# Attention values in portions of two query tiles, narrower first scores, and a last norm that goes tile by tile

## The chip, the cores and the metric

The kernel runs on one core of a Trainium2 chip. Such a core has five engines with instruction streams of their own: TensorE (PE) multiplies matrices into PSUM, VectorE (DVE) and ScalarE (ACT) do elementwise work, GpSimd (POOL) does small elementwise work and issues transfers, and SyncE (SP) issues transfers. They wait for one another by semaphores. The metric is the device time of one execution in microseconds (us). The program runs on one core, so the slowest core is the only one.

## The reference

One step of a decoder with one layer computes 512 prompt tokens and 8 x 8 sample tokens, 576 columns in all, at a width of 1024:

```python
h = _rmsnorm(x, norm1_g) * (1.0 + sc1) + sh1
proj = h @ w_in                       # b_gate, c_gate, xa, q, k, v, ga, gb
u = c_gate * xa
uc, new_conv = _causal_conv(u, conv_buf, conv_w)
ya = (b_gate * uc) @ w_conv_out
o, k_state, v_state = attend(q, k, v, attn_sinks)
yb = o @ w_attn_out
mixed = jax.nn.sigmoid(ga) * ya + jax.nn.sigmoid(gb) * yb
x = x + g1 * (mixed @ w_mix_out)
h2 = _rmsnorm(x, norm2_g) * (1.0 + sc2) + sh2
a, val = jnp.split(h2 @ w_up, 2, axis=-1)
ac, new_ffn = _causal_conv(a, ffn_buf, ffn_conv_w)
x = x + g2 * ((jax.nn.gelu(ac, approximate=False) * val) @ w_down)
...
y_prompt = _rmsnorm(xp, final_g)
y_sample = _rmsnorm(xs, final_g)
```

The attention of the prompt works in blocks of 128 queries. A block sees its own 128 keys and the 128 before them, with a distance penalty, a mask and a sink in the softmax; the first block has no keys before it:

```python
s = jnp.einsum('...qhgd,...khd->...hgqk', q, k) * (HEAD_DIM ** -0.5)
s = s - _alibi_slopes()[:, :, None, None] * dist[..., None, None, :, :]
s = jnp.where(valid[..., None, None, :, :], s, NEG_INF)
m = jnp.maximum(jnp.max(s, axis=-1, keepdims=True), sink)
p = jnp.exp(s - m)
p = p / (jnp.sum(p, axis=-1, keepdims=True) + jnp.exp(sink - m))
return jnp.einsum('...hgqk,...khd->...qhgd', p.astype(v.dtype), v)
```

There are 16 query heads of width 64 in 4 groups, each group with one key and value head.

## The kernel before

Activations lie transposed: 128 channels on the partitions, the 576 tokens along the free dimension, one tile for each of the eight channel blocks. Weights come from DRAM in blocks of eight 128 x 128 pieces (`load_w`, line 148). So that the products are as exact as float32, each operand is split into a high and a low part of the type fp32r (`split`, line 138: ScalarE copies the high part, VectorE subtracts), and each product is made in three passes, high x high, high x low and low x high (`kstep`, line 206). A plain `product` (line 218) does so for eight pieces and two column groups of 256 and 320 tokens (`GRP`). A `pair_product` (line 449) makes two output blocks of 128 channels at once by a scheme with seven parts in place of eight, on sums of weights and of activations; its columns are halves of 288 tokens. The weights of such a pair (a `Job`, line 1288) are made by `prepare` (line 1298) in steps named A, B, C and D, each with a high and a low part. For a letter in `moved` the low part is not a subtraction on VectorE: ScalarE writes the negated high part, and a transfer that GpSimd issues adds the raw weights to it (`low`, line 409).

The kernel goes through these stages: the first norm; the keys and values; six `PLAIN` blocks of the inner convolution (line 1429), made by plain products; 18 jobs of pair products; the attention's output products; the mixing; the second norm; the up-projections with their convolution; the down-projections; the final norm and the stores.

Beside the plain products runs a filler (`fill`, `tick`, lines 186 to 199): a generator that advances by a step for each so many pieces of a product. It holds the attention first (line 1149). `attention()` has 16 units, four key heads by four query blocks. At step n it makes the scores of unit n (`prompt_scores`, line 1095), advances by one yield, makes the values of unit n - 3 (`prompt_values`, line 1131) and turns the softmaxed scores of unit n - 2 (`prompt_turn`, line 1116). For the first unit of a head it waits until the head's queries are there and 8 ticks old.

- `prompt_scores` makes eight matmuls for a unit: four query heads, each with the high and with the low part of the keys. High and low parts of a query lie in the two halves of the partitions, which a transfer on GpSimd's queue puts there (`queries`, line 903). Each is 256 keys wide, for the first query block too, which has only 128 keys.
- `prompt_turn` transposes the scores, 128 x 128 at a time, into one or two tiles of 512 columns that ScalarE copies out of PSUM.
- `prompt_values` multiplies with the values. A weight piece is only 64 columns wide, so that two matmuls go to the two halves of the PSUM partitions. Float32 matmuls that are not fp32r are issued as two instructions each. A unit has two or four matmuls, 4 or 8 instructions; ScalarE then copies 256 columns into the attention's output tile `ot`.

PSUM is given out as two pairs of banks (`mmps`) and four single banks (`aux`). What sets the order: a planner orders the instructions of each engine by a simulated timeline. Instructions of engines in the list `pinned` are tied behind the one issued before on their engine; PE is in it from line 968, ScalarE and VectorE too from line 1465. The first matmul of `prompt_values` is not tied, so that the planner may place it, with everything tied behind it, ahead of scores that are not ready.

In the last plain step (line 1461) the weights of job 0 are prepared between the product's pieces. Each convolution of an inner block (`branch_conv`, line 1377) is one GpSimd copy, one ScalarE multiplication and two VectorE operations over 592 columns; that of block 6 is done in job 0, at step 3. Job 2 is its first reader.

At the end, the last two down-projection blocks are made in column groups of their own. `summed` (line 2071) squares an output block on ScalarE, adds the square to `acc3` on VectorE and scales the block by the norm's weight on ScalarE. `final_rows` (line 2083) sums `acc3` over the partitions by matmuls with a tile of ones, one for each token tile, and raises the sums to the power of -1/2 (`rows_rsqrt`, line 577: one VectorE and one GpSimd instruction). A `TokenTile` (line 1749) transposes a tile of 128 tokens back, `finish` scales it by that factor, 512 channels on ScalarE and 512 on VectorE, and stores both halves. Token tiles 2 and 3 are finished while the last product runs (`others`, line 2186). Token tile 4 holds the 64 sample tokens.

Of the kernel before, what the change touches and what calls it, by code (L numbers as in the profile page):

```python
# [16 lines left out]
P = 128  # L17
# [55 lines left out]
def step_kernel(ctx: ExitStack, tc: tile.TileContext, ins: dict, outs: list):  # L73
# [766 lines left out]
    def vt(i):  # L840
        return V[i // 2][:, i % 2, :]
# [253 lines left out]
    def prompt_scores(hd, i):  # L1095
        w = 256 if i else P
        k0 = (i - 1) * P if i else 0
        ss = [slot("s", shape=[P, 2, 256]) for _ in range(2)]
        kh, kl = (x[:, k0 : k0 + 256] for x in KS[hd])
        for x in range(2):  # L1100
            S = aux()
            for e in range(2):
                q = QS[4 * hd + 2 * x + e][:, i * P : i * P + P]
                dst = S[:, e * 256 : e * 256 + 256]
                matmul(dst, q, kh, start=True, stop=False)
                matmul(dst, q, kl, start=False, stop=True)
# [21 lines left out]
            pts.append(t)  # L1128
        return pts

    def prompt_values(hd, i, pts):
        nkt = len(pts)
        O = aux()
        for n in range(2 * nkt):
            kt, par = n // 2, n % 2
            done = nc.tensor.matmul(  # L1136
                O[HALF[par], :256],
                vt(i - nkt + 1 + kt)[:, hd * 64 : hd * 64 + 64],
                pts[kt][:, par * 256 : par * 256 + 256],
                start=(kt == 0), stop=(kt == nkt - 1),  # L1140
            )
            if n:
                tc.keep_in_program_order(done)
        nc.scalar.copy(
            ot[hd // 2][:, 2 * (hd % 2) : 2 * (hd % 2) + 2, i * P : i * P + P],
            O[:, :256].rearrange("p (g c) -> p g c", g=2),
        )

    def attention():
        units = [(hd, i) for hd in range(4) for i in range(4)]  # L1150
        s, pts = {}, {}
        for n in range(len(units) + 3):
            if n in CACHE_AT:
                cache_load(CACHE_AT.index(n))
            if n < len(units):
                hd, i = units[n]
                while 4 * hd + 3 not in QS or ticks[0] < ready[hd]:
                    yield False
                s[n] = prompt_scores(hd, i)
            yield False  # L1160
            if n >= 3:
                prompt_values(*units[n - 3], pts.pop(n - 3))
            if 2 <= n <= len(units) + 1:
                pts[n - 2] = prompt_turn(units[n - 2][1], s.pop(n - 2))
            yield False
        filler[1] = .35
        before = None
        for n in range(3):
            s, more = [], []
            if n < 2:  # L1170
                yield from decode_scores(n, s, more)
            if before is not None:
                yield from before
            before = decode_values(n, s, more)
# [254 lines left out]
    for at, m in enumerate(PLAIN):  # L1429
        if at in (4, 5):  # L1430
            src, dst = ((ins["cache_k_win"], nks), (ins["cache_v_win"], nvs))[at - 4]
            tc.keep_in_program_order(
                nc.gpsimd.dma_start(
                    dst[:, 0:120, :].rearrange("b (x w) c -> b x (w c)", x=2),
                    src[0].rearrange("b w h d -> b w (h d)")[:, 8:128, :].rearrange(
                        "b (x w) c -> b x (w c)", x=2
                    ),
                )
            )
        if 1 <= at <= 3:  # L1440
            key_parts(at)
            for t in (2 * at, 2 * at + 1):
                queries(t)
        w = weights(kpm(w_in, 1024 + m * P), NK)
        if at in (4, 5):
            operands(2 * at - 8)
        if at == 5 and filler:
            filler[1] = .4
        ps = product(w, h)
        if at == 0:  # L1450
            stT = state_in(st_conv, "stT", NK)
        if at == 1:
            a = aux()
            transpose(a[:, :74], par2, ident[:74, :74])
            nc.scalar.copy(par2T, a[:, :74])
        c_sb = slot("c")
        nc.scalar.copy(c_sb, ps)
        w = weights(kpm(w_in, 2048 + m * P), NK)
        if at in (4, 5):
            operands(2 * at - 7)  # L1460
        steps = {}
        if at == len(PLAIN) - 1:
            jobs[0].load()
        if at == len(PLAIN) - 1:
            pinned += [pe, act, dve]
            fs = [f for x in jobs[0].prepare("BD").values() for f in x]
            for k, n in [(0, 2), (1, 1), (2, 1), (3, 1), (4, 2), (5, 1), (6, 1), (7, 1)]:
                steps[k], fs = fs[:n], fs[n:]
            jobs[1].load()
        ps = product(w, h, steps)  # L1470
        u = padded()
        dve.tensor_tensor(out=u[:, 2:514], in0=pv(ps), in1=pv(c_sb), op=ALU.mult)
        dve.tensor_tensor(
            out=b10(u)[:, :, 2:10], in0=b8(sv(ps)), in1=b8(sv(c_sb)), op=ALU.mult
        )
        keep_state(u, m, NK)
        inner[m] = lambda u=u, m=m: branch_conv(u, m)
        if at < len(PLAIN) - 1:
            inner[m]()
# [9 lines left out]
    def g_list(names):  # L1489
        return [g_at(int(n[0]), n[1:]) for n in names.split()]  # L1490

    jobs[0].before = {2: [op.n3 for op in hp], 3: [lambda: inner[6]()]}
    jobs[7].before = {2: [lambda: inner[3]()]}
    jobs[8].before = {2: [lambda: inner[7]()]}
    jobs[9].before = {2: [lambda: state_out(NK, ncv_p[:], ncv_s[:])]}
# [253 lines left out]
    class TokenTile:  # L1749
# [14 lines left out]
        def finish(self, queues):  # L1764
            r, i = self.rows, self.i
            out = [slot("yo", shape=[P, 512]) for _ in range(2)]
            fr = r3[r, i : i + 1]
            act.activation(out[0][r], self.ps[0][r], AF.Copy, scale=fr)
            if i == 4:
                act.activation(out[1][r], self.ps[1][r], AF.Copy, scale=fr)  # L1770
            else:
                dve.tensor_scalar(
                    out=out[1][r], in0=self.ps[1][r], scalar1=fr, scalar2=None, op0=ALU.mult
                )
            for hh, queue in enumerate(queues):
                cs = slice(hh * 512, hh * 512 + 512)
                dst = y_p[0, i * P : i * P + P, cs] if i < 4 else y_s.flatten_outer_dims()[:, cs]
                queue.dma_start(dst, out[hh][r])
# [289 lines left out]
    acc3 = slot("acc")  # L2068
    r3 = cp.tile([P, 8], F32, tag="r3", name="r3")

    def summed(m, c0=0, c1=NT, last=False):

        sq = acc3 if m == 0 else slot("sq")
        act.activation(sq[:, c0:c1], x1[m][:, c0:c1], AF.Square)
        if m and not last:
# [5 lines left out]
        return sq  # L2081

    def final_rows(g, sq=None):

        a = mmps()
        i0, i1, step = (0, 2, 512) if g == 0 else (2, 5, 2)
        parts = [acc3] if sq is None else [acc3, sq]
        for n, x in enumerate(parts):
            for i in range(i0, i1):
                dst = a[:, (i - i0) * step : (i - i0) * step + 2]  # L2090
                matmul(dst, tok_cols(x, i), ones[:, 0:2], start=n == 0, stop=n == len(parts) - 1)
        src = a[:, : (i1 - i0) * step].rearrange("p (i e) -> p i e", e=step)[:, :, 0]
        rows_rsqrt(r3[:, i0:i1], src)
# [80 lines left out]
    def down_late(m, g, between=None):  # L2174
        ps = product_g(late[m - NK + LATE], fa, g, mmps(), between)
        residual(ps, x1[m], 40 + m, *GRP[g])
        return summed(m, *GRP[g], last=(m, g) == (NK - 1, 0))

    for m in range(NK - LATE, NK):
        down_late(m, 1)  # L2180
# [3 lines left out]
    pinned.extend([pe, act, dve])  # L2184

    def others():
        final_rows(1)
        for i in (2, 3):
            tt = TokenTile(i)
            tt.turn(range(NK))  # L2190
            tt.finish((nc.sync, nc.sync))

    sq = down_late(NK - 1, 0, (3, others))
    tt = TokenTile(4)
    tt.turn(range(NK))
    tt.finish((nc.sync, nc.sync))
    final_rows(0, sq)
    for i, last in ((0, nc.sync), (1, nc.scalar)):
        tt = TokenTile(i)
        tt.turn(range(NK))  # L2200
# [35 lines left out]
```

## Time and profile before

| what | value |
|---|---|
| median of three runs | 966.99 us (966.77 to 967.02) |
| the profiled execution | 968.06 us |
| its span | 966.2 us |
| mean granted TensorE clock | 0.996 of full speed |
| TensorE busy | 950.6 us, 98% |
| VectorE busy | 710.5 us, 74% |
| ScalarE busy | 540.9 us, 56% |
| GpSimd busy | 131.8 us, 14% |
| moved by transfers | 144.61 MB, mean 150 GB/s |

All times of the profile count from the start of the span. Engines: PE is TensorE's matmul stream and PEld its weight loads, which overlap the matmuls. A row of the timeline gives the start, the length, the engine, the line, the operation, output <- input, the shape and a count of merged instructions. In brackets, where there is one, stands how long the engine was idle before and what released it. Most operations are recorded by one helper and so have line 112; they are told apart by their tiles. Matmuls overlap, so that the time one of them takes from the others is read from start to start, not from its length. In the page, a line of 40 digits gives the busy share of an engine in 40 slices of the span, in tenths.

### The profile page before, as it was taken

How to read it: one execution, taken by the hardware profiler on the slowest of the kernel's cores; microseconds unless marked ns; L12 is line 12 of the kernel's file. 1: busy time of each engine (PE TensorE's matmuls, PEld its weight loads, DVE VectorE, ACT ScalarE, POOL GpSimd, SP SyncE). 2: the span in 40 equal slices, each digit the busy share in tenths (PEclk: the TensorE clock that was granted, in tenths of full speed). 3: DMA queues.
4: the chain of work that ended last, by engine and by line, in shares of the span. 5: the costliest groups of instructions: out<-in, count | busy, mean ns of one | idle time of the engine just before them, and what ended most of it. 6: DMA issues, size and time to landing. Idle time of an engine off the chain costs nothing.

```text
span 966.2 us, 18732 instructions
## 1 busy us (share of the span) xinstructions
PE 950.6 (98%) x7326; PEld 913.5 (95%) x7326; DVE 710.5 (74%) x1330; ACT 540.9 (56%) x1021; POOL 131.8 (14%) x310
## 2 busy tenths in 40 slices
PE   7999999999999999999999999999999999999997
PEld 5799999898899989999889999999999999999997
DVE  4746777687865767876677688995559998968873
ACT  4454665558665446876335567564226565546664
POOL 2222112101211112210001131100000011101110
PEclk8999999999999999999999999999999999999999
DMA  9985332424655768899885742332333333328542
GB/s 276 326 253 147 90 85 71 130 87 119 154 139 160 242 215 214 209 248 268 300 285 131 169 109 66 89 103 73 101 91 93 88 88 103 89 78 175 131 90 99
DMA packets 182794, 144.61 MB, mean 150 GB/s; under 512 B 7704, under 2 KB 162140, under 8 KB 182418
## 3 DMA queue, kind: packets, MB, share of 16 engines
q1 hardware_dynamic: 172546, 111.72, 38.9%
q0 software_dynamic: 10016, 31.44, 14.3%
q8 instruction: 57, 0.93, 0.4%
q14 instruction: 31, 0.25, 0.1%
q10 hardware_dynamic: 144, 0.26, 0.1%
HBM read 113.89 MB, written 12.07 MB: 130 GB/s over the span
## 4 chain that ended last, share of the span: by engine, by line
PE 94%; DVE 2%; DMA 1%; ACT 1%; issue 0%; SPq 0%; POOL 0%; POOLq 0%; DVEq 0%; ACTq 0%
PE mm L112 54%; PE aux L112 37%; PE aux L1232 2%; PE aux L1136 1%; DMA x<-in_x_prompt 1%; DMA q<-low 1%; SPq L497 0%; DVE wlo L112 0%; ACT whi L112 0%; DVE s L1048 0%; ACT hh L112 0%; DVE raw L112 0%; ACT junk L112 0%; DVE hl L112 0%; DVE y L112 0%
## 5 line engine op out<-in xcount | busy, mean ns | idle before, releaser
L112 ACT ACTIVATE whi<-raw 128x1024 fp32r<-128x1024 f32 (+3 forms) x183 | 185.7, 1022 | 104.0 <-PE mm L112 40.9
L112 DVE TENSOR_TENSOR wlo<-raw,whi 128x1024 fp32r<-128x1024 f32 (+3 forms) x159 | 187.3, 1184 | 45.9 <-ACT whi L112 45.1
L112 PE MATMUL mm<-hh,whi 128*128 128x256 f32 x336 | 74.0, 301 | 0.5 <-ACT hh L112 0.5
L112 PE MATMUL mm<-hh,wlo 128*128 128x256 f32 x336 | 71.6, 294 | 0.0
L112 PE MATMUL mm<-hl,whi 128*128 128x256 f32 x336 | 70.8, 295 | 0.1
L112 PE MATMUL aux<-2l,whi 128*128 128x288 f32 (+2 forms) x232 | 68.4, 295 | 0.0
L112 PE MATMUL aux<-2h,whi 128*128 128x288 f32 (+2 forms) x232 | 68.4, 295 | 0.0
L112 PE MATMUL aux<-2h,wlo 128*128 128x288 f32 (+2 forms) x232 | 68.3, 295 | 0.0
L112 DVE TENSOR_TENSOR raw<-raw 128x512 f32<-128x512 f32 x82 | 57.8, 705 | 2.7
L112 PEld LDWEIGHTS mm<-hh,whi 128*128 128x128 f32 x336 | 55.1, 188 | 1.9 <-ACT hh L112 1.1
L112 PEld LDWEIGHTS mm<-hh,wlo 128*128 128x128 f32 x336 | 56.2, 188 | 0.0
L112 PEld LDWEIGHTS mm<-hl,whi 128*128 128x128 f32 x336 | 55.5, 188 | 0.7 <-DVE hl L112 0.5
L112 PE MATMUL aux<-hh,whi 128*128 128x288 f32 (+2 forms) x184 | 53.9, 300 | 0.0
L112 PE MATMUL aux<-hl,whi 128*128 128x288 f32 (+2 forms) x184 | 52.9, 294 | 0.0
L112 PE MATMUL aux<-hh,wlo 128*128 128x288 f32 (+2 forms) x184 | 52.8, 294 | 0.0
L112 PE MATMUL mm<-nh,whi 128*128 128x288 f32 x164 | 48.9, 298 | 0.2 <-DVE g L112 0.2
L112 PE MATMUL mm<-th,whi 128*128 128x288 f32 x164 | 49.1, 300 | 0.0
L112 PE MATMUL aux<-th,whi 128*128 128x288 f32 x164 | 48.6, 296 | 0.0
L112 PE MATMUL mm<-th,wlo 128*128 128x288 f32 x164 | 48.5, 295 | 0.0
L112 PE MATMUL aux<-th,wlo 128*128 128x288 f32 x164 | 48.4, 295 | 0.0
L112 PE MATMUL mm<-nl,whi 128*128 128x288 f32 x164 | 48.4, 295 | 0.0
L112 PE MATMUL mm<-nh,wlo 128*128 128x288 f32 x164 | 48.4, 295 | 0.0
(374 smaller groups left out, 3015.5 us busy)
## 6 DMA issues: line engine op xcount, KB each, us to landing
raw<-in_w_in SPq DMA_DIRECT2D x52, 512.0 KB, 4.9
raw<-in_w_up SPq DMA_DIRECT2D x44, 512.0 KB, 4.0
ada<-in_w_ada SPq DMA_DIRECT2D x64, 256.0 KB, 5.3
wlo<-raw POOLq DMA_DIRECT2D x18, 512.0 KB, 4.6
ad<-in_w_ada SPq DMA_DIRECT2D x32, 256.0 KB, 6.6
raw<-in_w_down SPq DMA_DIRECT2D x16, 512.0 KB, 4.2
sg_dram<-sg POOLq DMA_DIRECT2D x16, 288.0 KB, 4.3
gt<-sg_dram SPq DMA_DIRECT2D x16, 288.0 KB, 5.5
```

The costliest lines, as they stand in the source:

```text
L112: done = getattr(self.engine, name)(*args, **kwargs)
L1136: done = nc.tensor.matmul(O[HALF[par], :256], vt(i - nkt + 1 + kt)[:, hd * 64 : hd * 64 + 64], pts[kt][:, par * 256 : par * 256 + 256], st ...
L1232: done = nc.tensor.matmul(ps[32 * j : 32 * j + 32, :], cT[:, k, :], cols[k][j], start=(k == 1), stop=(k == NK - 2),)
```

## The change

- Prompt values are made for two units in one portion. At the even steps n from 4 on, the values of units n - 4 and n - 3 are made back to back into the two halves of one PSUM bank, and two ScalarE copies follow. At odd steps no values are made. Only the first matmul of a portion is left untied. The loop still has 19 steps.
- The scores of the first query block of each head are 128 keys wide.
- In the last plain step, job 0 is prepared with "D" moved alone; the low part of B becomes a VectorE subtraction.
- The convolution of block 6 goes from step 3 of job 0 to step 3 of job 1.
- The second half of token tile 4 is scaled by VectorE instead of ScalarE.
- After the last product, token tiles 0 and 1 go on their own: the residual and the square of each tile of 128 columns, then the scaling by the norm's weight, on VectorE instead of ScalarE. Tile 4's first five transposes stand ahead of the sums and its other three behind them. The sums of the two tiles lie in two single banks, and each is raised by its own `rows_rsqrt`.

```diff
@@ prompt_scores
-        kh, kl = (x[:, k0 : k0 + 256] for x in KS[hd])
+        kh, kl = (x[:, k0 : k0 + w] for x in KS[hd])
...
-                dst = S[:, e * 256 : e * 256 + 256]
+                dst = S[:, e * 256 : e * 256 + w]
@@ prompt_values
-    def prompt_values(hd, i, pts):
-        nkt = len(pts)
+    def prompt_values(parts):
         O = aux()
...
+        for u, (hd, i, pts) in enumerate(parts):
+            nkt, c = len(pts), slice(256 * u, 256 * u + 256)
+            for n in range(2 * nkt):
+                kt, par = n // 2, n % 2
+                done = nc.tensor.matmul(
+                    O[HALF[par], c],
+                    vt(i - nkt + 1 + kt)[:, hd * 64 : hd * 64 + 64],
+                    pts[kt][:, par * 256 : par * 256 + 256],
+                    start=(kt == 0), stop=(kt == nkt - 1),
+                )
+                if u + n:
+                    tc.keep_in_program_order(done)
+        for u, (hd, i, pts) in enumerate(parts):
+            nc.scalar.copy(
+                ot[hd // 2][:, 2 * (hd % 2) : 2 * (hd % 2) + 2, i * P : i * P + P],
+                O[:, 256 * u : 256 * u + 256].rearrange("p (g c) -> p g c", g=2),
             )
@@ attention
-            if n >= 3:
-                prompt_values(*units[n - 3], pts.pop(n - 3))
+            if n >= 4 and n % 2 == 0:
+                prompt_values([(*units[u], pts.pop(u)) for u in (n - 4, n - 3)])
@@ last plain step, jobs
-            fs = [f for x in jobs[0].prepare("BD").values() for f in x]
+            fs = [f for x in jobs[0].prepare("D").values() for f in x]
...
-    jobs[0].before = {2: [op.n3 for op in hp], 3: [lambda: inner[6]()]}
+    jobs[0].before = {2: [op.n3 for op in hp]}
+    jobs[1].before = {3: [lambda: inner[6]()]}
@@ TokenTile.finish
-            if i == 4:
-                act.activation(out[1][r], self.ps[1][r], AF.Copy, scale=fr)
-            else:
-                dve.tensor_scalar(
-                    out=out[1][r], in0=self.ps[1][r], scalar1=fr, scalar2=None, op0=ALU.mult
-                )
+            dve.tensor_scalar(
+                out=out[1][r], in0=self.ps[1][r], scalar1=fr, scalar2=None, op0=ALU.mult
+            )
@@ summed, final_rows
-    def summed(m, c0=0, c1=NT, last=False):
+    def summed(m, c0=0, c1=NT):
...
-    def final_rows(g, sq=None):
+    def final_rows():
         a = mmps()
...
+        for i in range(2, 5):
+            matmul(a[:, 2 * i : 2 * i + 2], tok_cols(acc3, i), ones[:, 0:2], start=True, stop=True)
+        rows_rsqrt(r3[:, 2:5], a[:, 4:10].rearrange("p (i e) -> p i e", e=2)[:, :, 0])
@@ the end
-    sq = down_late(NK - 1, 0, (3, others))
-    tt = TokenTile(4)
-    tt.turn(range(NK))
-    tt.finish((nc.sync, nc.sync))
-    final_rows(0, sq)
+    m = NK - 1
+    ps = product_g(late[-1], fa, 0, mmps(), (3, others))
+    spans = [(i * P, i * P + P) for i in range(2)]
+    sq, x = slot("sq"), x1[m]
+    for c0, c1 in spans:
+        residual(ps[:, c0:c1], x, 40 + m, c0, c1)
+        act.activation(sq[:, c0:c1], x[:, c0:c1], AF.Square)
+    for c0, c1 in spans:
+        dve.tensor_scalar(
+            out=x[:, c0:c1], in0=x[:, c0:c1], scalar1=par2T[:, 66 + m : 67 + m], scalar2=None, op0=ALU.mult
+        )
+    t4, sums = TokenTile(4), [aux() for _ in range(2)]
+    t4.turn(range(5))
+    for parts in (acc3, sq):
+        for i in range(2):
+            matmul(sums[i][:, :2], tok_cols(parts, i), ones[:, 0:2], start=parts is acc3, stop=parts is sq)
+    t4.turn(range(5, NK))
+    for i in range(2):
+        rows_rsqrt(r3[:, i : i + 1], sums[i][:, :1])
+    t4.finish((nc.sync, nc.sync))
```

More of the change, by code (lines that the diff above doesn't have):

```diff
@@ L1129, in prompt_turn @@
         return pts
-    def prompt_values(hd, i, pts):
-        nkt = len(pts)
+    def prompt_values(parts):
         O = aux()
[L1134 to L1140, printed above, removed]
-            )
[L1142 to L1146, printed above, removed]
-        )
+        for u, (hd, i, pts) in enumerate(parts):
[14 more added lines that the diff above has]
+                O[:, 256 * u : 256 * u + 256].rearrange("p (g c) -> p g c", g=2),
+            )
     def attention():
@@ L2069, in step_kernel @@
     r3 = cp.tile([P, 8], F32, tag="r3", name="r3")
-    def summed(m, c0=0, c1=NT, last=False):
+    def summed(m, c0=0, c1=NT):
         sq = acc3 if m == 0 else slot("sq")
         act.activation(sq[:, c0:c1], x1[m][:, c0:c1], AF.Square)
-        if m and not last:
+        if m:
             dve.tensor_tensor(
@@ L2080, in summed @@
         act.activation(x, x, AF.Copy, scale=par2T[:, 66 + m : 67 + m])
-        return sq
-    def final_rows(g, sq=None):
+    def final_rows():
         a = mmps()
[L2086 to L2093, printed above, removed]
+        for i in range(2, 5):
+            matmul(a[:, 2 * i : 2 * i + 2], tok_cols(acc3, i), ones[:, 0:2], start=True, stop=True)
+        rows_rsqrt(r3[:, 2:5], a[:, 4:10].rearrange("p (i e) -> p i e", e=2)[:, :, 0])
     late, wd_raw = [], {2: raw[2], 3: raw[3]}
@@ L2176, in down_late @@
         residual(ps, x1[m], 40 + m, *GRP[g])
-        return summed(m, *GRP[g], last=(m, g) == (NK - 1, 0))
+        summed(m, *GRP[g])
     for m in range(NK - LATE, NK):
@@ L2186, in others @@
     def others():
-        final_rows(1)
+        final_rows()
         for i in (2, 3):
```

1 line of the change is left out of this document (removed).

## The prediction

> **What bounds the kernel now.** I read the page's first two parts, then its chain of work that ended last, then the timeline of TensorE, VectorE and ScalarE at the places that the change touches.
>
> ```profile
> span 966.2 us, 18732 instructions
> PE 950.6 (98%) x7326; PEld 913.5 (95%) x7326; DVE 710.5 (74%) x1330; ACT 540.9 (56%) x1021; POOL 131.8 (14%) x310
> ...
> PE   7999999999999999999999999999999999999997
> ...
> PE 94%; DVE 2%; DMA 1%; ACT 1%; issue 0%; SPq 0%; POOL 0%; POOLq 0%; DVEq 0%; ACTq 0%
> ```
>
> TensorE is busy in every slice but the first and the last, and 94% of the chain is its own. So a TensorE instruction that takes less shortens the run by as much, work on VectorE, ScalarE and GpSimd costs only where TensorE comes to wait for it, and the last slice goes by the latency from the last product to the stores.
>
> The profiled execution took 968.06 us, of which 966.2 is the span and 1.9 lies around it; the median of the runs is 966.99, 1.1 less. I make the sum as a difference, so 968.06 and 966.99 move alike, and give the result against the median.
>
> **The change part by part.**
>
> **1. Values, two query tiles a portion.** The same 112 instructions and 16 ScalarE copies run, in 8 portions instead of 16. What changes is how often TensorE goes from full-width products to the half-width value matmuls and back to transposes. Timeline of TensorE (start, length, line, operation, count):
>
> ```profile
> 97.32 0.43 PE L112 MATMUL mm<-hh,wlo 128*128 128x256 f32 x2
> 97.58 0.60 PE L112 MATMUL aux<-ident,s 128*128 128x128 f32 x4
> 97.94 0.51 PE L112 MATMUL mm<-hh,whi 128*128 128x256 f32 x2
> ...
> 104.27 0.42 PE L112 MATMUL mm<-hh,wlo 128*128 128x256 f32 x2
> 104.62 0.65 PE L1136 MATMUL aux<-pt,V 128*64 128x256 f32 x4
> 105.20 1.09 PE L112 MATMUL aux<-ident,s 128*128 128x128 f32 x8
> ...
> 160.95 1.08 PE L1136 MATMUL aux<-pt,V 128*64 128x256 f32 x8
> 161.97 1.09 PE L112 MATMUL aux<-ident,s 128*128 128x128 f32 x8
> ...
> 170.50 0.66 PE L112 MATMUL aux<-ident,s 128*128 128x128 f32 x4
> 170.91 0.51 PE L112 MATMUL mm<-hh,whi 128*128 128x256 f32 x2
> ```
>
> The same pair of products holds TensorE for 0.26 us when transposes follow (97.32 to 97.58) and for 0.35 when values follow (104.27 to 104.62): 0.09 to enter. A portion of four takes 0.58 (104.62 to 105.20), one of eight 1.02 (160.95 to 161.97), so four more cost 0.44 and eight at that rate 0.88: 0.14 more inside a portion, however long. Four transposes behind values take 0.41 (170.50 to 170.91), behind products 0.36 (97.58 to 97.94): 0.05. Together 0.28 a portion; 8 portions fewer give 8 x 0.28 = -2.2 us. Bounds: -2.2 and, should each query tile pay its own entry inside the joined portion, 0. I take -2.2, since the rows show one fixed cost whatever the length. The copies and the later release of the bank lie beside products.
>
> **2. The wait for the queries of head 3.** Moving unit 8's values from the step before the first scores of head 3 to behind them takes cover away. Timeline of TensorE, and one row of ScalarE:
>
> ```profile
> 176.81 0.65 PE L1136 MATMUL aux<-pt,V 128*64 128x256 f32 x4
> ...
> 184.21 0.28 PE L112 MATMUL aux<-kl,q 128*128 128x256 f32 x1
> 185.15 0.36 PE L112 MATMUL aux<-kh,q 128*128 128x256 f32 x1 [0.66 <-DMA q<-low]
> 185.34 0.28 PE L112 MATMUL aux<-kl,q 128*128 128x256 f32 x1
> 185.55 1.08 PE L1136 MATMUL aux<-pt,V 128*64 128x256 f32 x8
> ```
> ```profile
> 176.83 1.18 ACT L896 ACTIVATE q<-mm 64x512 fp32r<-64x512 f32 x2
> ```
>
> The fifth score waits for the transfer of a query half: 185.15 less 184.21 less a normal step of 0.12 is 0.8 us. The copies that begin that half's way start at 176.83, when its product is done, so the value portion at 176.81 lies between product and scores. Without it TensorE is at the scores 0.58 + 0.09 + 0.05 = 0.7 earlier, the transfer lands when it did, and the wait grows by 0.7. What else the portions save before this point moves product and transfer alike. Bounds: +0.7, and -0.8 if the planner, which is free to place the first value matmul of a portion, puts the joined portion ahead of the fifth score; in before it stands behind six scores, so I take +0.7. Queued behind the waiting score are all later products.
>
> **3. First scores over 128 keys.** Four units with 8 matmuls each: 32 matmuls go from 256 to 128 columns. Timeline rows of the scores' step, and of narrower instructions near the end:
>
> ```profile
> 173.39 0.28 PE L112 MATMUL aux<-kh,q 128*128 128x256 f32 x1
> 173.51 0.28 PE L112 MATMUL aux<-kl,q 128*128 128x256 f32 x1
> ...
> 957.19 0.59 PE L112 MATMUL mm<-ones,sq 128*128 128x2 f32 x4
> 957.64 1.94 PE L112 MATMUL aux<-ident,x 128*128 128x128 f32 x16
> ```
>
> A score takes 0.12 now. Matmuls of two columns take (957.64 - 957.19) / 4 = 0.11 each, transposes of 128 columns about (1.94 - 0.27) / 15 = 0.11. So 0.11 is what one instruction with 128 weight columns takes however narrow its moving side is, and the weight load is what remains: 32 x 0.01 = -0.2 us with the rounding (0.118 to 0.111). No row has this operand kind (fp32r) under 256 columns. Bounds: half the step, -1.9; or twice 0.11 a matmul, as plain fp32 takes, which issues two instructions for each (four records for the two sums in the row above): 32 x 0.10 = +3.2. I take -0.2: the rows at 2 and 128 columns are the nearest. [...]
>
> **4. The last plain step and job 0.** B's low part is made by VectorE (one subtraction of 1.2 us) and no longer by a ScalarE copy of 1.06 and an accumulating transfer on GpSimd's queue. The convolution of channel block 6 (0.8 on ScalarE, 1.7 on VectorE, a small GpSimd copy, no DMA) goes from job 0 to job 1. Timeline of VectorE, ScalarE, TensorE:
>
> ```profile
> 232.59 1.23 DVE L112 TENSOR_TENSOR wlo<-raw,whi 128x1024 fp32r<-128x1024 f32 x1 [2.01 <-ACT whi L112]
> 241.25 1.71 DVE L112 SCALAR_TENSOR_TENSOR y<-pad,parT,y 128x592 f32<-128x592 f32 x2
> 245.35 0.45 DVE L112 TENSOR_TENSOR g<-mm,p 128x288 f32<-128x288 f32 x1
> 256.24 0.46 DVE L112 TENSOR_TENSOR g<-mm,p 128x288 f32<-128x288 f32 x1 [1.66 <-ACT kTc L1025]
> ```
> ```profile
> 229.12 1.06 ACT L112 ACTIVATE wlo<-whi 128x1024 fp32r<-128x1024 f32 x1
> 240.43 0.78 ACT L112 ACTIVATE y<-pad,parT 128x592 f32<-128x592 f32 x1
> ```
> ```profile
> 245.19 0.29 PE L112 MATMUL aux<-hl,whi 128*128 128x288 f32 x1
> 245.33 0.29 PE L112 MATMUL aux<-hh,wlo 128*128 128x288 f32 x1
> 245.85 0.40 PE L112 MATMUL mm<-nh,whi 128*128 128x288 f32 x1 [0.23 <-DVE g L112]
> ```
>
> VectorE idles 2.0 us before 232.59, so the subtraction is hidden; if ScalarE's cover goes, it delays the next sums, which are first needed half a job later. In job 0 the product at 245.85 starts 0.52 after the one before instead of 0.14 (245.19 to 245.33), because `g` at 245.35 came late behind the 1.71 of taps: moving them gives -0.4. In job 1 they meet an idle of 1.66 before 256.24, which takes all but 0.05 of the 1.71. Queued behind them there are the next weights' sums and a softmax, whose readers come later. Bounds: -0.4 and +0.4 (the same wait in job 1). I take -0.4.
>
> **5. The tail.** Timeline of the end:
>
> ```profile
> 956.15 0.48 DVE L112 SCALAR_TENSOR_TENSOR x<-mm,modT,x 128x256 f32<-128x256 f32 x1 [0.66 <-PE mm L112]
> 956.67 0.42 ACT L112 ACTIVATE sq<-x 128x256 f32<-128x256 f32 x1 [1.32 <-DVE x L112]
> 957.82 0.16 DVE L112 TENSOR_SCALAR r<-mm 128x2 f32<-128x2 f32 x1 [1.18 <-PE mm L112]
> 958.05 0.69 POOL L112 TENSOR_TENSOR r<-r,mhalf 128x2 f32<-128x2 f32 x1 [4.00 <-DVE r L112]
> 958.82 1.55 DVE L112 TENSOR_SCALAR yo<-aux,r 128x512 f32<-128x512 f32 x2 [0.84 <-POOL r L112]
> 954.80 6.38 SPq L1778 DMA_DIRECT2D out<-yo  x9
> ```
>
> By halves the residual and the square of the first tile are done some 0.4 us sooner (half of 0.48 and of 0.42), so its raising starts at about 957.6 instead of 958.05 and ends by 958.3; the second raising ends at about 959.0. But the last transposes end at 957.64 + 1.94 = 959.58 as before, and the last scaled half tile (0.75) at about 960.37 as before. What moves is the queue of stores: it ends at 961.18, 0.8 after the last half tile, of which about 0.4 is the issue itself and 0.4 waiting behind earlier stores. With tile 4's and tile 0's stores earlier, the last one starts as soon as its data is there: at most -0.4. Scaling tile 4's half on VectorE (0.75) lies where VectorE waited 0.84 for GpSimd; an equal slip gives +0.4 as the other bound. I take -0.3.
>
> **Sum.** -2.2 + 0.7 - 0.2 - 0.4 - 0.3 = -2.4 us: 965.7 for the profiled execution, 964.6 for the median.
>
> **The rivals.**
>
> A. The planner puts the joined portion ahead of the waiting score. Then the 0.8 of the wait goes instead of 0.7 coming: -2.4 - 1.5 = -3.9, 963.1 us. For it: the fifth score reaches its place earlier, so in the plan too its transfer may not have landed. Against: six scores stood ahead in before.
>
> B. Narrow fp32r matmuls pass as plain fp32. The place is the 32 scores, the price 3.2 instead of -0.2; it turns the whole into a loss once a score takes more than 0.118 + (2.4 - 0.2) / 32 = 0.19 us. -2.4 + 3.4 = +1.0: 968.0 us, slower than before. For it: every fp32r product in the profile has at least 256 columns, so nothing excludes it. Against: the 0.11 of the narrow rows.
>
> C. Joining does nothing: the fixed cost is paid for each query tile, or the planner's new order brings waits of the same size. Then -0.2 + 0.7 - 0.4 - 0.3 = -0.2: 966.8 us. Against: portions of four and eight share one fixed cost.
>
> [...]
>
> **How the numbers follow.** Forecast 0.44 (its own range 963.5 to 965.8), A 0.22, B 0.12, C 0.15, D 0.07. The range from 962.5 to 967.9 leaves out about 1 in 10: the low end is A with half a us of other waits gone, the high end B. A measurement of this kernel can tell about 0.2%, 1.9 us, from no change, so faster means under 965.1. Two thirds of the forecast lie there, and nearly all of A and D: 0.29 + 0.22 + 0.07 = 0.58. Slower, over 968.9, are the upper part of B and of C: 0.10. Same: 0.32.
>
> **What would show it.** Part 1: eight value portions of 12 or 16 instructions, each with one gap at entry, and eight sets of transposes straight behind products. Part 2: the idle before the fifth score of head 3, 1.5 us or none. [...] Part 4: no idle before `mm<-nh` of job 0, and none new in job 1. Part 5: the raising by single columns, and the last store's issue straight behind the last half tile. The prediction is wrong if the narrow scores take over 0.19, or if the planner's new order puts new waits into the attention stage from 100 to 230 us.

## The result, and the profile after

The changed kernel takes 963.16 us, the median of six runs (962.46 to 963.90), against 966.86 for the kernel before in six runs beside them. The ratio of the two is 0.9963 with a 95% interval of 0.9950 to 0.9976: 3.7 us faster, between 2.3 and 4.8. The forecast was 964.6 us, 2.4 faster, with 962.5 to 967.9 as its range.

The page of the changed kernel, for the lines shown of before:

```profile
span 961.7 us, 18733 instructions
PE 947.5 (99%) x7326; PEld 913.7 (95%) x7326; DVE 713.4 (74%) x1336; ACT 538.3 (56%) x1019; POOL 132.0 (14%) x310
...
PE   7999999999999999999999999999999999999997
...
PE 95%; DMA 3%; ACT 0%; DVE 0%; issue 0%; DVEq 0%; SPq 0%
```

The bound is the same, TensorE. Its busy time fell by 3.1 us (950.6 to 947.5) and the span by 4.5. This profiled run took 963.44 us and that of before 968.06, so the two profiles lie 4.6 apart where the medians lie 3.7 apart; the runs of one kernel lie 1.4 us apart here and up to 3.7 in the experiments. A good part of this spread probably comes from the first 84 us, where all kernels do nearly the same work: there the fourteen profiles, one of each kernel, lie up to 3.5 us apart. So profiles are compared from 84 us on below, and a wait that one pair of profiles shows is looked for in the others.

Comparing the start of every product in the two traces, most of the difference comes about between 85 and 265 us: the joined portions, and four waits (at head 3, at 235, 245 and 263 us). The stage around the first scores of head 3, TensorE's timeline after:

```profile
181.73 0.43 PE L112 MATMUL mm<-hh,wlo 128*128 128x256 f32 x2
182.00 0.22 PE L112 MATMUL aux<-kh,q 128*128 128x128 f32 x1
182.06 0.27 PE L112 MATMUL aux<-kl,q 128*128 128x128 f32 x1
182.17 0.28 PE L112 MATMUL aux<-kh,q 128*128 128x128 f32 x1
182.28 0.27 PE L112 MATMUL aux<-kl,q 128*128 128x128 f32 x1
182.47 0.30 PE L112 MATMUL aux<-kh,q 128*128 128x128 f32 x1
182.61 0.28 PE L112 MATMUL aux<-kl,q 128*128 128x128 f32 x1
182.81 1.51 PE L1137 MATMUL aux<-pt,V 128*64 128x256 f32 x12
```

Three things stand in it. The portion of twelve has one start and one end. The narrow scores go at 0.11 a step (182.06 to 182.17 to 182.28). And the fifth score waits 0.08 (182.47 less 182.28 less 0.11), where before it waited 0.8 and the forecast had 1.5.

### The profile page after: what moved, and what is told of

Read it like the earlier page. It is cut to its first block, busy times and chain, and to the rows that moved or that the text cites. A ratio compares the mean times of both kernels' runs of the same rounds, so it can differ in the third digit from the quotient of the medians.

```text
span 961.7 us, 18733 instructions
## 1 busy us (share of the span) xinstructions
PE 947.5 (99%) x7326; PEld 913.7 (95%) x7326; DVE 713.4 (74%) x1336; ACT 538.3 (56%) x1019; POOL 132.0 (14%) x310
## 4 chain that ended last, share of the span: by engine, by line
PE 95%; DMA 3%; ACT 0%; DVE 0%; issue 0%; DVEq 0%; SPq 0%
PE mm L112 55%; PE aux L112 37%; PE aux L1234 2%; DMA ad<-in_w_ada 1%; PE aux L1137 1%; DMA raw<-in_w_in 1%; DMA x<-in_x_prompt 0%; ACT whi L112 0%; ACT wlo L112 0%; DVEq L2241 0%; SPq L497 0%; DVE cs L504 0%; ACT hh L112 0%; DVE hl L112 0%; ACT yo L112 0%
## 5 line engine op out<-in xcount | busy, mean ns | idle before, releaser
L112 DVE TENSOR_TENSOR wlo<-raw,whi 128x1024 fp32r<-128x1024 f32 (+2 forms) x160 | 188.7, 1186 | 49.2 <-ACT whi L112 48.3
```

What stands on the lines that cost most here:

```text
L112: done = getattr(self.engine, name)(*args, **kwargs)
```

## The experiments

All kernels were timed against the kernel before in five rounds, the whole change in its own six runs. The microseconds are the ratio less 1, times 967.6, which is about the median of before in the rounds (967.4 to 967.8).

| what is in the kernel | median, us | ratio (95%) | us against before |
|---|---|---|---|
| 1: joined portions alone | 969.21 | 1.0015 (1.0006 to 1.0024) | +1.5 |
| 3: narrow scores alone | 968.29 | 1.0005 (0.9996 to 1.0014) | +0.5 |
| 4: last plain step and job 0 alone | 964.25 | 0.9970 (0.9960 to 0.9980) | -2.9 |
| 5: tail alone | 967.59 | 0.9999 (0.9990 to 1.0008) | -0.1 |
| B's low part on VectorE alone | 966.95 | 0.9995 (0.9987 to 1.0004) | -0.5 |
| 1 with B's low part on VectorE | 966.00 | 0.9980 (0.9972 to 0.9989) | -1.9 |
| 1 and 4 | 963.46 | 0.9954 (0.9943 to 0.9966) | -4.5 |
| the whole change | 963.16 | 0.9963 (0.9950 to 0.9976) | -3.6 |

### Each part alone

The portions alone are the pieces `prompt_values` and `attention` of the diff; the scores alone are `kh, kl` and `dst` cut to `w`; the fourth part alone is

```
-            fs = [f for x in jobs[0].prepare("BD").values() for f in x]
+            fs = [f for x in jobs[0].prepare("D").values() for f in x]
...
-    jobs[0].before = {2: [op.n3 for op in hp], 3: [lambda: inner[6]()]}
+    jobs[0].before = {2: [op.n3 for op in hp]}
+    jobs[1].before = {3: [lambda: inner[6]()]}
```

and the tail alone is everything from `finish` down. Expected of the four, in this order:

> Only the joined value portions. By the prediction's terms: eight portions fewer give -2.2 us, and the wait for the queries of head 3 grows by 0.7: -1.5 in all. By the traces of before and after: the growth of the wait came to nothing because VectorE made the low half of those queries 1.74 us earlier, 0.6 more than TensorE had gained by then; if joining alone brings that order, -2.2 to -3.0 and a wait under 0.3; if it came from the narrow scores, -1.5 and a wait of about 1.5. Rival (joining does nothing): 0.

> Only the scores over 128 keys. Prediction: 32 steps of 0.111 for 0.118, -0.2 us. [...] The planner may move other work, which I put at up to 0.5 either way.

> Only the last plain step without B's low part and the convolution of block 6 in the second job. Prediction: -0.4 us, the wait before job 0's products over `nh` (step 0.52) gone, none new in the second job. Rival (the same wait turns up in the second job): 0 to +0.4. If the wait of 0.4 for VectorE at the start of the last fifty us before the end (901 us) also goes by this, -0.8.

> Only the tail. Prediction: -0.3 us. By the trace of after, where VectorE's last half tile ended 0.5 later behind the last product than before, because its half of the sample tile waited for ScalarE's: +0.3 to +0.5.

The portions alone made the kernel slower (+1.5, interval +0.6 to +2.3), which neither theory had; the wait at head 3 was 1.00 in this run, between the two values that they named. The fourth part alone brought 2.9 where at most 0.8 was expected. Scores and tail can't be told from nothing. Added up the four give about -1, not -3.6: the parts are not independent. Joining alone, TensorE's timeline and then the row of GpSimd's queue and the stretches around (stretch, its length, TensorE's busy time, granted clock, share of DMA, GB/s; a packet counts where it starts, so that the share can pass 1):

```profile
232.20 0.29 PE L112 MATMUL aux<-tl,whi 128*128 128x288 f32 x1
235.60 0.40 PE L112 MATMUL aux<-th,wlo 128*128 128x288 f32 x1 [3.10 <-DMA wlo<-raw]
...
237.17 0.44 PE L112 MATMUL aux<-th,whi 128*128 128x288 f32 x1
237.41 0.44 PE L112 MATMUL aux<-tl,whi 128*128 128x288 f32 x1
...
240.44 0.29 PE L112 MATMUL mm<-tl,whi 128*128 128x288 f32 x1
240.57 0.29 PE L112 MATMUL mm<-th,wlo 128*128 128x288 f32 x1
```
```profile
230.45 0.97 POOL L112 DMA_DIRECT2D wlo<-raw  x1 [16.97 <-PE mm L112]
```
```profile
236.60:237.10 0.50, 0.50 (x5) 0.85 1.19 227
237.10:240.10 3.00, 3.00 (x29) 0.50 0.93 218
240.10:240.60 0.50, 0.50 (x5) 0.73 0.21 59
```

In the profile of this run TensorE has gained 2.1 us on before from 85 to 230 us, and is 2.8 ahead of it in all. It then arrives at job 0's first product with B's low part, which an accumulating transfer is still making: issued at 230.45, in before at 230.49, it lands 5.1 us later (4.7 in before), at 235.6. TensorE stands for 3.1 us, and then runs at half its clock until 240.4: 0.24 a step (237.17 to 237.41) in place of 0.13 (240.44 to 240.57). From 230 to 240 the run loses 4.6: 3.3 by the stop (232.20 to 235.60, less a step of 0.13) and 1.3 by the slow steps. That is all that joining had brought, and more.

Why the transfer was issued no earlier, though TensorE was 2.8 us ahead, stands in ScalarE's rows. Joining alone, then before:

```profile
227.10 0.59 ACT L1127 COPY pt<-aux 128x512 f32<-128x512 f32 x1 [2.22 <-PE aux L1137]
...
228.54 0.64 ACT L1146 COPY o<-aux 128x256 f32<-128x256 f32 x2
229.06 1.08 ACT L112 ACTIVATE wlo<-whi 128x1024 fp32r<-128x1024 f32 x1
```
```profile
226.96 1.06 ACT L1127 COPY pt<-aux 128x512 f32<-128x512 f32 x2
...
231.23 0.37 ACT L1144 COPY o<-aux 128x256 f32<-128x256 f32 x1 [0.52 <-PE aux L1136]
```

With joined portions a copy of the last turned scores waits 2.22 us for the values portion, and this portion's two output copies stand ahead of the negated copy to which the transfer adds. In before there is no such wait (226.96), and the output copy comes behind (231.23). So joining makes TensorE earlier and holds ScalarE's share of B's low part where it was (229.06, in before 229.12). The same 2.22 us stand in the profiles of the changed kernel and of all others with portions of two, where VectorE makes the part; no run keeps the transfer and takes this wait away, so its share in the stop is read from the rows alone.

In before the same transfer was just in time. The first product that reads it, who waited for what makes or reads `wlo` from 230 to 241 us of before (the landing line covers two transfers), and the issue:

```profile
234.96 0.30 PE L112 MATMUL aux<-tl,whi 128*128 128x288 f32 x1
235.21 0.40 PE L112 MATMUL aux<-th,wlo 128*128 128x288 f32 x1
```
```profile
who waited for it (us, times):
  PEld aux L112: 0.2, 1
...
DMA to landing us min/median/max: 4.7/4.9/5.2
```
```profile
230.49 0.97 POOL L112 DMA_DIRECT2D wlo<-raw  x1 [14.09 <-ACT wlo L112]
```

Issued at 230.49 it landed 4.7 later, at 235.2, and the first product that reads it started at 235.2 as well, 0.25 behind the product before where a step is 0.13: no slack at all, and 0.1 of a wait already. This step is 0.25 and 0.26 in the runs of tail and scores alone, and 0.13 or 0.14 wherever VectorE makes the part.

### Is it that transfer?

One more piece on top of the portions (the `"D"` line above), block 6 left in job 0:

> Joined value portions, and B's low part in the last plain step made by VectorE; the convolution of block 6 stays in the first job. Theory after the first runs: joining alone lost 4.6 us at 232 because TensorE came 2.8 us earlier to B's low part, whose transfer landed when it did before; without the transfer that wait is gone, so against joining alone -4.6, and against before -2.2 to -2.8 (964.6 to 965.6 where before has 967.8). Rival (the 3.4 us wait has another cause, as the planner's order around 232): within 1 us of joining alone, slower than before.

Measured: -1.9 against before, -3.4 (by the ratios, within 1.2) against joining alone, so that the rival falls. VectorE makes the part itself, and the wait is gone. A smaller one comes in its place, which the -4.6 of the theory left out. VectorE, then TensorE, of this run:

```profile
229.89 1.23 DVE L112 TENSOR_TENSOR wlo<-raw,whi 128x1024 fp32r<-128x1024 f32 x1 [1.92 <-ACT whi L112]
```
```profile
243.62 0.29 PE L112 MATMUL aux<-hh,wlo 128*128 128x288 f32 x1
245.23 0.40 PE L112 MATMUL mm<-nh,whi 128*128 128x288 f32 x1 [1.32 <-DVE g L112]
```

The step before job 0's products over `nh` is 1.61 here and 0.52 in before: VectorE now does this subtraction as well as the taps of block 6 ahead of `g`. So the 1.2 us on VectorE were covered in the forecast by an idle time that lay ahead of them, but not what stood behind them.

> Only B's low part on VectorE; portions, scores, block 6 and tail as before. Theory (in before the transfer lands just in time, so it is a bound only when TensorE comes earlier): no gain of its own; the subtraction of 1.2 us makes `g` of the first job later, so 0 to +1.1 us. Rival (the transfer cost time in before already): -1 or more.

B's low part on VectorE without the portions: -0.5 with an interval of -1.3 to +0.4. It has no gain of its own; its profile shows the same grown wait for `g`, 0.87 idle where before has 0.23.

> Joined value portions and the whole of the fourth part (B's low part on VectorE, block 6 in the second job); scores and tail as before. Theory: the two parts support each other, -2.2 to -2.8 for the portions on top of -2.9 for the fourth part alone: -4.5 to -5.5, at least as fast as the whole change. Rival (the parts add up as measured alone, +1.4 and -2.9): -1.5.

With block 6 in the second job as well it is -4.5, the near end of what the theory had and far from the rival's -1.5. The step before `mm<-nh` is 0.14 (242.63 to 242.77 in this run), and a second wait goes that the forecast hadn't seen. The decode scores of 263 us waited for VectorE's sums over the tile of the scores before; of before, TensorE and VectorE:

```profile
263.11 0.84 PE L112 MATMUL aux<-kTc,qS 64*32 64x128 f32 x16 [0.41 <-DVE s L1048]
```
```profile
261.45 1.22 DVE L112 TENSOR_TENSOR wlo<-raw,whi 128x1024 fp32r<-128x1024 f32 x1
262.58 0.87 DVE L1048 SCALAR_TENSOR_TENSOR s<-con,aux 128x256 f32<-128x256 f32 x2
```

After, VectorE's order is another one:

```profile
258.17 0.87 DVE L1048 SCALAR_TENSOR_TENSOR s<-con,aux 128x256 f32<-128x256 f32 x2
258.95 0.68 DVE L112 TENSOR_TENSOR raw<-raw 128x512 f32<-128x512 f32 x1
259.55 1.22 DVE L112 TENSOR_TENSOR wlo<-raw,whi 128x1024 fp32r<-128x1024 f32 x1
```

The planner put the sums ahead of the low part, and TensorE's idle time is gone. This gives 0.6 in the pair of profiles. The wait is gone in every run with block 6 in the second job, and there in every run without.

### The width of the scores

```
-                matmul(dst, q, kh, start=True, stop=False)
-                matmul(dst, q, kl, start=False, stop=True)
+                for c in range(0, w, 64 if w == P else w):
+                    cs = slice(c, c + 64 if w == P else w)
+                    matmul(dst[:, cs], q, kh[:, cs], start=True, stop=False)
+                    matmul(dst[:, cs], q, kl[:, cs], start=False, stop=True)
```

> The whole change, but each of the 32 narrow scores is cut into two of 64 columns, 64 matmuls in place of 32. Theory (a narrow score takes its weight load, 0.11, whatever its width): 32 more by 0.11 = +3.5 us against the whole change, and steps of 0.11 between scores of 64 columns. Rival (the time goes by columns, as by half a step): 0, steps of 0.06.

Its ratio to before is 0.9991 (0.9983 to 1.0000), to the whole change +2.7 us (1.2 to 4.2). The steps:

```profile
82.33 0.28 PE L112 MATMUL aux<-kh,q 128*128 128x64 f32 x1
82.44 0.28 PE L112 MATMUL aux<-kl,q 128*128 128x64 f32 x1
82.55 0.28 PE L112 MATMUL aux<-kh,q 128*128 128x64 f32 x1
```

0.11 at 64 columns as at 128, against 0.12 at 256. From 128 columns to 64 the width no longer counts; what is left is the time of an instruction with 128 weight columns, and cutting a score in two costs a whole one. In the trace of after the weight loads of the 128-column scores start 0.11 apart as well (182.00, 182.11 and 182.22, each 0.19 long).

### Longer portions

As the run with 1 and 4, but four query tiles a portion, in two banks (the call is shown):

```
-            if n >= 4 and n % 2 == 0:
-                prompt_values([(*units[u], pts.pop(u)) for u in (n - 4, n - 3)])
+            if n >= 6 and n % 4 == 2:
+                prompt_values([(*units[u], pts.pop(u)) for u in range(n - 6, n - 2)])
```

> Portions and fourth part as in the run that had both, but four query tiles a portion: four portions in place of eight. Theory (0.28 us a portion, whatever its length): 4 x 0.28 = -1.1 us more, -5.5 against before. Rival (the longer portion keeps VectorE and ScalarE waiting, or the wait for the queries of head 3 comes back): no faster than -4.4, with new idle time of TensorE between 100 and 230 us.

967.87 us, ratio 1.0000 (0.9991 to 1.0008): 4.5 slower than portions of two. The rival holds. Its TensorE timeline has the new waits:

```profile
148.01 0.36 PE L112 MATMUL aux<-kh,q 128*128 128x256 f32 x1 [0.69 <-DMA q<-low]
...
182.80 0.36 PE L112 MATMUL aux<-kh,q 128*128 128x256 f32 x1 [0.86 <-DMA q<-low]
...
229.42 1.14 PE L1138 MATMUL aux<-pt,V 128*64 128x256 f32 x8 [2.22 <-ACT pt L1127]
```

The last portion comes up before ScalarE has copied its last turned scores, and the queries of heads 2 and 3 come late. With these three (0.85, 0.2 more than before, and 2.5 by the steps) taken off, the stage from 85 to 230 us is 3.1 shorter than in before, for twelve portions fewer: 0.26 a portion, near the 0.28 of the forecast. Up to 230 us this run falls 3.6 us behind the portions of two; where the rest of the 4.5 goes stays open.

### The tail

Three forms of it on the changed kernel: the tail of before; the sample tile's two halves in two tiles; both halves on ScalarE as in before. The edit of the second, and the start of that of the third:

```
-            self.ps = [aux() for _ in range(2)] if mm is None else [mm[:, :512], mm[:, 512:]]
+            self.ps = [aux() for _ in range(2)] if mm is None else [mm[:, :512], mmps()[:, :512]]
```
```
+            if i == 4:
+                act.activation(out[1][r], self.ps[1][r], AF.Copy, scale=fr)
+            else:
+                dve.tensor_scalar(
```

> The whole change, but the sample tile's two halves stand in two tiles of the pool, so that VectorE's half waits for the transposes and no longer for ScalarE's half. Theory (this wait of 0.9 us is what the tail lost): VectorE's last half tile ends 0.5 to 0.7 us earlier behind the last product, the kernel 0.3 to 0.7 faster than the whole change. Rival (the end is set by the store on ScalarE's queue, whose issue took 2.3 us): no change, 0.0.

> The whole change with the tail of before. Theory (the new tail is worth nothing or loses 0.3): -3.7 to -4.4 against before, at most 0.5 faster than the whole change. Rival (the new tail gains its 0.3): 0.3 slower than the whole change.

> The whole change, but both halves of the sample tile are scaled by ScalarE, as before. Theory (VectorE's wait for ScalarE's half is what the tail lost): VectorE begins the last two half tiles as soon as GpSimd's raising is done, and the last half tile ends 0.3 to 0.4 us earlier behind the last product; the time is up to 0.4 better than the whole change. Rival (the last store's issue sets the end): 0.0.

Measured ratios to before: two tiles 0.9963 (0.9951 to 0.9975), old tail 0.9957 (0.9943 to 0.9970), ScalarE 0.9958 (0.9945 to 0.9970), all beside the 0.9963 of the whole change. In time none of the tails can be told from another. In the traces they can. VectorE, ScalarE and its queue of the whole change:

```profile
953.77 0.76 DVE L112 TENSOR_SCALAR yo<-mm,r 64x512 f32<-64x512 f32 x1 [0.94 <-ACT yo L112]
954.57 1.41 DVE L112 TENSOR_SCALAR yo<-aux,r 128x512 f32<-128x512 f32 x2
```
```profile
953.06 0.68 ACT L112 ACTIVATE yo<-mm,r 64x512 f32<-64x512 f32 x1 [0.86 <-PE mm L112]
...
955.15 2.33 ACTq L1778 DMA_DIRECT2D out<-yo  x1
```

and VectorE with the sample tile on ScalarE:

```profile
953.36 1.62 DVE L112 TENSOR_SCALAR yo<-aux,r 128x512 f32<-128x512 f32 x2 [1.17 <-PE aux L112]
```

From the start of the last product (950.93 after, 950.28 in this run) VectorE's last half tile ends 5.05 later after, 4.70 with the sample tile on ScalarE, and 4.54 with the old tail (the same in before). So the half tile on VectorE with its wait for ScalarE's half is 0.35 of the 0.5 that the new tail lost; the edit takes the wait and the work away together and doesn't part them. Giving it two tiles took that wait away but brought others of 0.36 and 0.39, since the second tile comes free only with the residual; its half tile ends at 5.15, and the experiment settles nothing. The time from the start of the last product to the end of the span is 10.2 to 10.7 in the five profiles with a new tail (mean 10.5). In the nine with the old one it is 9.5 to 9.7 in seven and 10.4 and 10.6 in two, of which the profile of before is one (mean 9.8). So by the traces the new tail loses about 0.7, twice the 0.35 that the pair of before and after shows. The store on ScalarE's queue took 0.4 to 0.9 us to issue in the nine, and 1.5 to 2.3 in four of the five; why, no run tells.

## Why the prediction came out as it did

The time was in the range, faster was the likeliest case, and the sum of -2.4 against -3.7 measured (-2.3 to -4.8) is just inside the interval. The terms behind it were not all right, one thing that carries the result was not in it, and that the sum came out so near is in part luck.

**1. Portions, -2.2: right in size, but not on its own.** From 85 to 230 us, with the wait for head 3 taken off, the runs with joining alone, with B's low part and with the fourth part gained 2.3 each: 0.29 a portion. What the engine does in the 0.28 or 0.29 us that a portion costs, no trace shows. The step that failed is "a TensorE instruction that takes less shortens the run by as much": 2.2 us on TensorE's side are worth nothing while a transfer further on keeps its place. And "the copies and the later release of the bank lie beside products" put at nothing the 2.22 us that ScalarE came to wait for the last joined portion, ahead of its share in that transfer. The forecast said of B's low part only that the subtraction is hidden, and never asked when the transfer that it replaces lands and who is there then. With the fourth part in the same change it was not to be seen; alone, the portions lose.

**2. The wait for the queries of head 3, +0.7: wrong.** The step that failed here is "the transfer lands when it did". The portion is gone from between the product and the scores, as the forecast has it, but the planner also moved work on VectorE: in before, four scalings of a softmax (1.14 us) stood ahead of the low half of these queries, and after they stand behind. Before, then after:

```profile
174.73 1.14 DVE L994 TENSOR_SCALAR s<-s,den 128x256 f32<-128x256 f32 x4
...
178.77 0.67 DVE L899 SCALAR_TENSOR_TENSOR low<-mm,q 64x512 fp32r<-64x512 f32 x1
```
```profile
177.03 0.68 DVE L899 SCALAR_TENSOR_TENSOR low<-mm,q 64x512 fp32r<-64x512 f32 x1
...
180.64 0.62 DVE L994 TENSOR_SCALAR s<-s,den 128x256 f32<-128x256 f32 x2
```
```profile
179.98 0.52 POOL L903 DMA_DIRECT2D q<-low  x1 [7.49 <-DVE qX L907]
```
```profile
178.25 0.52 POOL L903 DMA_DIRECT2D q<-low  x1 [6.61 <-issue]
```

From this transfer's issue to the fourth score it is 4.23 in before (179.98 to 184.21) and 4.03 after (178.25 to 182.28): 0.2 less, not 0.7. It is 4.16 to 4.23 in all runs without joining and 4.00 to 4.10 in all with it, so joining alone brings that order. How long TensorE waits then goes by the flight of the transfer. With the same order of work the wait was 0.82, 1.19, 0.39, 0 and 0 in the five profiles without joining (mean 0.48), and 0.08, 1.00, 0.75, 0.03, 0.31, 0.51 and 0.58 in seven with joining (mean 0.47; the longer portions and the cut scores are left out). So the 0.74 that the pair of profiles shows in favour of the change is one draw, and the term is about 0. Rival A's outcome, no wait, turned up in a few runs without its cause: the portion stands behind six scores as in before.

**3. Narrow scores, -0.2: right.** The step is 0.11, and 0.06 once for the first behind a product. The four runs with joined portions and scores of 128 columns gain 2.7 from 85 to 230 us, with the wait at head 3 taken off, where those with joined portions and 256 columns gain 2.3. Rival B (as plain fp32, slower) falls by the steps, and by the times as well: the scores alone gave +0.5, between -0.4 and +1.4, where B has +3.2. The 0.07 under D in the chances is for a shorter step; no run shows one, the narrow scores go at 0.11 at 128 columns and at 64.

**4. The last plain step and job 0, -0.4: the mechanism right, the term much too small.** The wait before `mm<-nh` went as forecast. Not forecast were the wait of 0.6 at 263 us and about 0.4 at 901 us, where VectorE's order before a residual changed; and the whole of the interaction. The 0.4 at 901 us is not bound to this part: joining alone has lost half of it, and the run with 1 and 4 keeps 0.25. The fourth part alone is worth 2.9 us by the times, and on top of the portions 5.9 (1.0015 to 0.9954). In its own profile the fourth part alone gains 2.9 from 84 to 950 us as well: 0.4 at head 3, which is a draw (see 2), 0.2 at B's low part, 0.4 before `mm<-nh`, 0.9 at 263 us, 0.4 at 901, and 0.6 in small steps whose cause stays open. So only some 1.5 us of the 2.9 are traced to this part.

**5. The tail, -0.3: wrong in sign by the traces, not decided by the times.** What came in the pair of before and after is the "equal slip" that the forecast had at +0.4 "as the other bound": the half on VectorE was to lie in a wait for GpSimd, but it began only when ScalarE had read its half of the same tile.

Put together from what the pair of before and after shows, with the draw at head 3 taken off: -2.3, about 0, -0.3, -0.4 - 0.6 - 0.4, and +0.4, which makes -3.6. That it meets the measured value so closely is partly chance, since the 0.4 at 901 us comes and goes, the 0.1 at B's low part is left out, and the tail's +0.4 is +0.7 over all profiles. The forecast fell short by about the two waits that it hadn't seen; its two wrong terms, +0.7 too much at head 3 and 0.7 too little in the tail, cancelled. Rival C (new waits eat what joining brings) is what happens without the fourth part.

No version beats the changed kernel by more than the measurement tells. The portions with the fourth part and nothing else (0.9954) and the changed kernel with the old tail (0.9957) are 0.9 and 0.6 us below its 0.9963, with intervals that overlap.

## What to carry to other kernels

Before crediting a saving on the engine that sets the time, list the transfers whose landing that engine meets in the next tens of microseconds and the slack of each; a transfer that lands just in time turns the saving into a wait (3.1 us with joining alone). A trace that shows almost no wait at such a place (0.1 in before) says nothing of how near it is: look for the issue, add the flight, and compare with the first reader. Ask too whether the change holds up the engine that prepares the transfer, as the joined portion held ScalarE here, for 2.22 us. And where a planner orders the work, a term that rests on one transfer's cover is worth its mean over several profiles, not the value in one.

## What the hardware showed that I had not expected

A stop of TensorE cost more than its length here. After 3.1 us of idle time (joining alone, 232.5 to 235.6; 3.4 from start to start of the matmuls) the granted clock fell to 0.50 about 1.4 us after work had begun again, and stayed there for about 3.4 us: 1.3 us on top of the stop. What brings the slow stretch and what sets its length, no run shows. After the 2.2 us of the longer portions there is none: the granted clock is 1.00 from 226 to 245 us of that run. Not every run of joining alone had it: 3.4 us at half the clock take 0.0018 off the mean, and the fastest of the eleven (967.43 us) has a mean granted clock of 0.999. How many of the others had it isn't shown; their median loses less (1.5) than the profile shows from 84 us on (2.4).

The flight of one and the same transfer of 64 x 512 differs by 0.7 us or more from run to run, in kernels whose work up to that place is the same. It lands 5.0 us after its issue in before, where the fifth score starts 5.17 after it; this score starts 4.73 after it in the run of the fourth part alone, and in those of the tail and of B's low part alone 4.35 after it, without a wait, so that the transfer was there by then. The wait was 0.82, 0.39, 0 and 0.
